# First layer of a two-part transformer: x first, modulation weights by column halves, projection pieces in between

## The chip, the core and the metric

The kernel runs on one core of a Trainium2 chip. The core has five engines that run side by side, each through its own instructions in order: TensorE (PE in the profile) multiplies matrices into PSUM, VectorE (DVE) and ScalarE (ACT) work element by element on SBUF and PSUM, GpSimd (POOL) on SBUF alone, and SyncE (SP) issues the loads and stores, which 16 DMA engines carry out. Semaphores order the engines. PE loads one operand as weights (PEld in the profile) and streams the other.

The metric is the device time of the whole program in microseconds, median of the runs. Lower is better.

## The reference

Six transformer layers over one sequence of 512 rows of 1024 float32 values. The first four are modulated by a condition c; the change concerns the start of the first of them:

```python
cond = jax.nn.silu(c)
for i in range(DEPTH):
    mod = (cond @ w_mod[i] + b_mod[i])[:, None, :]
    shift, scale, gate = jnp.split(mod, 3, axis=-1)
    h = rms_norm(x, norm_pre_g[i]) * (1.0 + scale) + shift
    ...
    o = gla_mixer(h, ...)
    ...
    x = x + gate * rms_norm(o, norm_post_g[i])
```

```python
def gla_mixer(h, w_in, w_a2, b_a, g_head, w_out):
    q, k, v, z, a_low = jnp.split(h @ w_in, [GLA_KD, 2 * GLA_KD, 2 * GLA_KD + GLA_VD, 2 * GLA_KD + 2 * GLA_VD], axis=-1)
    log_a = jax.nn.log_sigmoid((a_low @ w_a2 + b_a)) / GLA_NORMALIZER
    ...
```

`w_mod[0]` has 1024 rows and 3072 columns: 1024 of shift, 1024 of scale, 1024 of gate. `w_in` has 3088 columns; the values v of head 0 are columns 1024 to 1279. Two further layers (a second block with its own context sequence) follow and are not touched.

## The kernel before

One program computes everything, with x resident as four tiles of 128 rows. A planner at build time puts each engine's instructions in order from their place in the program and from simulated times; it also hands out the buffers of a pool, tag by tag in the order of the program (`NBUF`: 28 buffers of 4 KB per partition under "t4", 10 under "t2", 5 raw weight pieces "wr", 4 each of their high and low parts "wh" and "wl").

`setup` (L139) loads the identity and a few columns, makes silu(c) (`condition`), and loads the shift and scale columns of `w_mod[0]` as 16 tiles of 128 rows by 1024 columns (512 KB each, k the block of rows, v shift or scale). x (`load_x`, four tiles of 512 KB) is issued after the eighth of them (L157). For each tile four matmuls with the condition as weights (L164; the profile counts eight) accumulate one row of shift and one of scale in PSUM. These rows are copied (L170), turned into columns by PE (L173) and joined with bias and norm weight (L178 to L182): `m` holds a scale and a shift for each of the 1024 features.

`first_block` (L2172) then normalises the four x tiles (`normed`, L518: squares on ScalarE, root on POOL, scaling on DVE and ScalarE) and calls `prenorm`'s step (L482). It transposes each pair or single tile on PE (L501), applies scale and shift out of PSUM (L507, L509) and splits the result into a high part that a fast matmul format holds and a low remainder (`split`, L254: copy on ScalarE, subtraction on DVE or POOL, L257). H, the normalised input with features on partitions, is eight blocks k of 128 features by 512 rows, high and low.

Then `gla` (L628) begins. It loads the head gain `gh` (L631) and projects head 0's values (`values`, `proj_tok` L288): four pieces of weights, each of two blocks k by 256 columns (256 KB, rows of 1 KB), each split into high and low; for each piece and each of four row tiles six matmuls (L310 to L312: high by high, high by low, low by high). That makes 96. Next are the decay (`gla_decay`, L667: three matmuls for each k with 16 columns, L675 to L677) and the queries and keys of head 0 (`proj_T`, L358 to L360).

Generators yield to a driver (`drain`, L423), which at each yield gives background work 0.6 of a step: the modulation rows of later layers (`mods`, L380; eight matmuls a tile, L393). `ADV = 1` lets the first piece of the values run ahead of the constants of the whole program (`consts`, L2153: some thirty small loads and two transposes of stacked columns, L228).

Of the kernel before, what the change touches and what calls it, by code (L numbers as in the profile page):

```python
# [21 lines left out]
D = 1024  # L22
# [54 lines left out]
class Core:  # L77
    def __init__(self, ctx, tc, A):
        self.ctx, self.tc, self.nc, self.A = ctx, tc, tc.nc, A
        pool = lambda name, bufs, **k: ctx.enter_context(tc.tile_pool(name=name, bufs=bufs, **k))  # L80
        self.cp = pool("const", 1)
        self.wp = pool("w", 3)
        self.mx = pool("mx", 2)
        self.sm = pool("sm", 4)
        self.dp = pool("dram", 1, space=DRAM)
        self.ps = pool("ps", 1, space=PSUM)
        self.turn = {}
        self.n = 0
        self.ph, self.nlo = "", {}
        self.bg, self.rate, self.owed = {"m": [], "c": []}, {"m": MRATE, "c": 0}, {"m": 0, "c": 0}  # L90
        self.two = "c_2" in A
        self.share = False
        self.sk = ""

# [44 lines left out]
    def setup(self):  # L139
# [13 lines left out]
        w = [self.t("t4", [128, D]) for _ in range(16)]  # L153
        for i, x in enumerate(w):
            k, v = i // 2, i % 2
            nc.sync.dma_start(x, A["w_mod"][0][k * 128:(k + 1) * 128, v * D:(v + 1) * D])
            if i == 7:  # L157
                self.load_x()
        pad = self.cond["c"]
        ps = [self.psA() for _ in range(2)]  # L160
        for i, x in enumerate(w):
            k, v = i // 2, i % 2
            for g in range(4):
                nc.tensor.matmul(ps[v][g * 32:(g + 1) * 32, :256], pad[:, k, :], x[:, g * 256:(g + 1) * 256],  # L164
                                 start=(k == 0), stop=(k == 7))
        m = self.small("mcol", [128, 16], bufs=3)
        bias = self.col("b_mod0", 16)
        for v in (1, 0):
            sb = self.t("t1", [128, 256])
            nc.vector.tensor_copy(sb, ps[v][:, :256])  # L170
            pt = self.psA()
            for h in range(2):
                nc.tensor.transpose(pt[:, h * 128:(h + 1) * 128], sb[:, h * 128:(h + 1) * 128], self.ident)  # L173

            col = pt[:, :256].rearrange("p (h g r) -> p g h r", h=2, r=32)[:, :, :, 0]
            o = m[:, 8 - 8 * v:16 - 8 * v].rearrange("p (g h) -> p g h", h=2)
            bv = bias[:, v * 8:v * 8 + 8].rearrange("p (g h) -> p g h", h=2)
            nc.vector.tensor_tensor(o, col, bv, op=ALU.add)  # L178
            if v:
                pre = self.small("pre0", [128, 8], bufs=1)  # L180
                nc.vector.tensor_scalar(pre, self.col("pre0", 8), 32.0, None, ALU.mult)
                nc.vector.scalar_tensor_tensor(m[:, 0:8], m[:, 0:8], 1.0, pre, ALU.add, ALU.mult)  # L182
        self.m0 = m
# [104 lines left out]
    def proj_tok(self, H, nt, W, K, c0, n, out, r0=0, each=None, inturn=False, lead=1, wide="pp"):  # L288
# [42 lines left out]
        for g in groups:  # L331
            ws = [(k0, nk, self.weights(W, r0 + k0, nk, c0, n)) for k0, nk in g]
# [295 lines left out]
    def gla(self, H, j, O):  # L628
        nc, A = self.nc, self.A
        W = A["gla_w_in"][j]  # L630
        gh = self.bcast(A["gla_g_head"][j].rearrange("h d -> (h d)"), 1024, "t4")  # L631
        nc.vector.tensor_scalar(gh, gh, 0.5, None, ALU.mult)
# [9 lines left out]
        for h in range(4):  # L642
            v = []
            if h == 0:

                yield from values(h, v)
                yield from self.gla_decay(H, j, b)
            o = []
# [1523 lines left out]
    def first_block(self, dst=None):  # L2172
        A, x = self.A, self.x
        H, step = self.prenorm(x, 4, self.m0)
        for t, xn in enumerate([self.normed(x(t)) for t in range(4)]):
            step(t, xn)
        if ADV == 0:
            self.consts()
        yield
        for i in range(4):  # L2180
# [3 lines left out]
            if i % 3 == 0:  # L2184
                gen = self.phase("gla", self.gla(H, i // 3, O))
                if i == 0 and ADV:

                    for _ in range(ADV):
                        next(gen)
                        yield  # L2190
# [32 lines left out]
ADV = 1  # L2223
# [69 lines left out]
```

## Time and profile before

| | us |
|---|---|
| median of 3 runs | 3271.91 |
| lowest, highest | 3269.6, 3280.09 |
| the profiled execution's own time | 3273.38 |
| its span in the profile | 3271.6 |
| PE busy in the span | 3099.9 |
| mean granted clock of PE | 0.975 of 2.4 GHz |

The profile is one execution. Its times are microseconds from the start of the span, single instructions in nanoseconds. In the tables by stages the engines stand in the order PE, PEld, DVE, ACT, POOL, each with its count. An engine that is busy is not always fast: a matmul's duration is modelled, and the distance between the starts of two matmuls says more of PE's pace. PEclk is the clock that was granted to PE in a stretch, 1.00 being 2.4 GHz and 0.50 being 1.2 GHz. A timeline merges equal neighbours and counts them (x8). Behind "<-" stands what an engine waited for.

### The profile page before, as it was taken

The page shows a single profiled execution, that of the slowest core. Times are in us where ns is not written, and L with a number is a line of the kernel's source. Part 1 is how long each engine was busy: PE and PEld are TensorE (multiplying, and loading weights), DVE is VectorE, ACT ScalarE, POOL GpSimd, SP SyncE. Part 2 cuts the span into 40 slices and gives each one's busy share as a digit, 9 for nine tenths or more (in the row PEclk, how much of TensorE's full clock was granted, in tenths as well). Part 3 has the DMA queues.
Part 4 walks back from the last instruction along what each step waited for, and adds up shares of the span by engine and source line. Part 5 has one row for each costly group of instructions (what it writes and reads, how often), then busy time and mean ns, then how long its engine had stood idle before and what let it go on. Part 6 is the DMA issues. An engine that isn't in the chain of part 4 may idle for free.

```text
span 3271.6 us, 61127 instructions
## 1 busy us (share of the span) xinstructions
PE 3099.9 (95%) x23487; PEld 2650.2 (81%) x23487; DVE 1691.7 (52%) x3554; ACT 1458.9 (45%) x3173; POOL 1306.4 (40%) x1312
## 2 busy tenths in 40 slices
PE   7999999999999999989999999899999989999998
PEld 4878889878877778878887789898888877888887
DVE  2744564454555564666897757651112468641112
ACT  3424544354544543345544544453323447643323
POOL 2544453232212345344543113554445341154445
PEclk9999999999989999999999999999999999999999
DMA  7355645754435625354564335353333330043332
GB/s 239 91 152 171 212 132 165 235 164 133 134 117 169 191 76 150 113 160 128 164 171 130 109 86 144 114 160 94 100 123 110 109 90 2 24 142 97 97 123 90
DMA packets 477420, 426.25 MB, mean 130 GB/s; under 512 B 108038, under 2 KB 421609, under 8 KB 477129
## 3 DMA queue, kind: packets, MB, share of 16 engines
q1 hardware_dynamic: 477129, 422.35, 43.0%
q8 instruction: 185, 3.03, 0.4%
q14 instruction: 106, 0.87, 0.1%
HBM read 383.66 MB, written 38.03 MB: 129 GB/s over the span
## 4 chain that ended last, share of the span: by engine, by line
PE 74%; DVE 10%; DMA 5%; ACT 4%; issue 3%; POOL 3%; SPq 1%; POOLq 0%; DVEq 0%; ACTq 0%
PE ffn.pp L359 6%; PE ffn.pp L358 6%; PE ffn.pp L360 6%; PE mods.pa L393 3%; PE out.pp L310 2%; PE out.pp L311 2%; PE out.pp L312 2%; PE ffn.pa L312 2%; PE ffn.pa L311 2%; PE ffn.pa L310 2%; DMA mods.wm<-in_w_mod_dram 2%; PE fox.pp L312 1%; PE fox.pp L311 1%; PE fox.pp L310 1%; PE sgu.pp L310 1%
## 5 line engine op out<-in xcount | busy, mean ns | idle before, releaser
L257 POOL TENSOR_TENSOR ffn.wl<-ffn.wr,ffn.wh 128x512 fp32r<-128x512 f32 x258 | 332.8, 1293 | 345.6 <-ACT ffn.wh L256 345.5
L256 ACT ACTIVATE ffn.wh<-ffn.wr 128x512 fp32r<-128x512 f32 x258 | 162.5, 631 | 348.3 <-PE ffn.pp L360 144.6
L358 PE MATMUL ffn.pp<-pre.t,ffn.wh 128*128 128x512 f32 x672 | 261.6, 389 | 0.0
L359 PE MATMUL ffn.pp<-pre.t,ffn.wl 128*128 128x512 f32 x672 | 261.4, 389 | 0.0
L360 PE MATMUL ffn.pp<-pre.t,ffn.wh 128*128 128x512 f32 x672 | 261.4, 389 | 0.0
L598 DVE SCALAR_TENSOR_TENSOR ffn.t<-ffn.t,ffn.pp 128x512 f32<-128x512 f32 (+1 forms) x66 | 39.4, 597 | 243.9 <-ACT ffn.t L597 243.9
L257 POOL TENSOR_TENSOR gla.wl<-gla.wr,gla.wh 128x512 fp32r<-128x512 f32 x66 | 86.9, 1317 | 162.1 <-ACT gla.wh L256 148.2
L310 PE MATMUL gla.pp<-gla.wh,pre.t 128*128 128x256 f32 x512 | 150.6, 294 | 0.8 <-ACT gla.t L651 0.4
L311 PE MATMUL gla.pp<-gla.wl,pre.t 128*128 128x256 f32 x512 | 149.9, 293 | 0.0
L312 PE MATMUL gla.pp<-gla.wh,pre.t 128*128 128x256 f32 x512 | 149.4, 293 | 0.5 <-DVE pre.t L257 0.4
L359 PEld LDWEIGHTS ffn.pp<-pre.t,ffn.wl 128*128 128x128 f32 x672 | 126.1, 188 | 26.3
L360 PEld LDWEIGHTS ffn.pp<-pre.t,ffn.wh 128*128 128x128 f32 x672 | 126.1, 188 | 26.1
L358 PEld LDWEIGHTS ffn.pp<-pre.t,ffn.wh 128*128 128x128 f32 x672 | 126.1, 188 | 26.0
L257 POOL TENSOR_TENSOR ffn.cwl<-ffn.cwr,ffn.cwh 128x512 fp32r<-128x512 f32 x44 | 60.8, 1382 | 213.8 <-ACT ffn.cwh L256 188.7
L393 PE MATMUL mods.pa<-mods.wm,cond_c 128*32 128x256 f32 x1408 | 122.5, 402 | 16.0 <-DMA mods.wm<-in_w_mod_dram 15.6
L1140 DVE SCALAR_TENSOR_TENSOR ffn.t<-ffn.t,ffn.pp 128x512 f32<-128x512 f32 (+1 forms) x66 | 39.4, 597 | 176.2 <-PE ffn.pp L360 175.5
L256 ACT ACTIVATE ffn.cwh<-ffn.cwr 128x512 fp32r<-128x512 f32 x132 | 82.9, 632 | 104.6 <-PE ffn.pp L360 39.6
L310 PE MATMUL sgu.pp<-sgu.wh,pre.t 128*128 128x256 f32 x384 | 112.6, 293 | 6.9 <-DVE gdnp.at L1267 6.0
L311 PE MATMUL ffn.pa<-ffn.wl,ffn.t 128*128 128x512 f32 x304 | 118.3, 389 | 0.0
L312 PE MATMUL ffn.pa<-ffn.wh,ffn.t 128*128 128x512 f32 x304 | 118.3, 389 | 0.0
L310 PE MATMUL ffn.pa<-ffn.wh,ffn.t 128*128 128x512 f32 x304 | 112.7, 389 | 0.0
L312 PE MATMUL sgu.pp<-sgu.wh,pre.t 128*128 128x256 f32 x384 | 110.8, 289 | 1.3 <-DVE pre.t L257 1.1
(823 smaller groups left out, 10719.7 us busy)
## 6 DMA issues: line engine op xcount, KB each, us to landing
mods.wm<-in_w_mod_dram SPq DMA_DIRECT2D x176, 512.0 KB
gla.wr<-in_gla_w_in_dram SPq DMA_DIRECT2D x96, 256.0 KB
ffn.wr<-in_w_ffn_gate_dram SPq DMA_DIRECT2D x88, 256.0 KB
ffn.wr<-in_w_ffn_up_dram SPq DMA_DIRECT2D x88, 256.0 KB
ffn.wr<-in_w_ffn_down_dram SPq DMA_DIRECT2D x88, 256.0 KB
fox.wr<-in_fox_w_in_dram SPq DMA_DIRECT2D x64, 256.0 KB
sgu.wr<-in_sgu_w_in_dram SPq DMA_DIRECT2D x48, 256.0 KB
out.res_x<-out.t SPq DMA_DIRECT2D x24, 512.0 KB
```

Source lines behind the costliest of these rows:

```text
L256: nc.scalar.activation(hi, src, AF.Copy)
L257: (lo_eng or nc.vector).tensor_tensor(lo, src, hi.bitcast(F32), op=ALU.subtract)
L310: nc.tensor.matmul(o, H.hi(kk, s), w[0][:, k], start=(kk == 0 and first), stop=False)
L311: nc.tensor.matmul(o, H.hi(kk, s), w[1][:, k], start=False, stop=False)
L312: nc.tensor.matmul(o, H.lo(kk, s), w[0][:, k], start=False, stop=(kk == K - 1 and last))
L358: nc.tensor.matmul(o, wh[:, k], H.hi(kk), start=(kk == 0), stop=False)
L359: nc.tensor.matmul(o, wl[:, k], H.hi(kk), start=False, stop=False)
L360: nc.tensor.matmul(o, wh[:, k], H.lo(kk), start=False, stop=(kk == K - 1))
L393: nc.tensor.matmul(ps[g * 32:(g + 1) * 32, :256], pad[:, j, :], ws[j][:, g * 256:(g + 1) * 256], start=(j == 0), stop=(j == 7))
L598: nc.vector.scalar_tensor_tensor(dst, dst, 1.0, z, ALU.add, ALU.mult)
L1140: nc.vector.scalar_tensor_tensor(f, sg, 0.5, o[1], ALU.mult, ALU.mult)
```

## The change

x is loaded ahead of the weights. The weights of shift and scale are loaded by column halves: a tile holds, for one block k, 512 columns of shift and the same 512 of scale (two rows of 2 KB on each partition, 512 KB in all). `setup` issues half 0, two pieces of the value projection, half 1, two more pieces. It normalises x, computes the columns of half 0 (`mods0`, `mods1`), and in between transposes the normalised x unscaled into `xT` (four tiles, eight copies out of PSUM by ScalarE and DVE in turn). The first two pieces are split there.

`first_block` makes the four blocks k of half 0 from `xT` (`norm0`: high part on ScalarE with scale and shift, the same in full on DVE, the difference on DVE or POOL), runs the value projection's first two pieces between the modulation matmuls of half 1, then makes the other four blocks and splits the last two pieces. After one yield come the constants and the rest. `proj_tok` takes pieces out of `self.early` before it loads any. The head gain's load in `gla` moves behind the decay.

```diff
--- before.py
+++ after.py
@@ -91,6 +91,7 @@
         self.two = "c_2" in A
         self.share = False
         self.sk = ""
+        self.early = []
 
     def nm(self, s):
         self.n += 1
@@ -150,37 +151,90 @@
         self.columns("cols0", [("c", r(A["c"]), 8), ("b_mod0", r(A["b_mod"][0:1, 0:2 * D]), 16),
                                ("pre0", r(A["norm_pre_g"][0:1]), 8)])
         self.condition("c", ("c",))
-        w = [self.t("t4", [128, D]) for _ in range(16)]
-        for i, x in enumerate(w):
-            k, v = i // 2, i % 2
-            nc.sync.dma_start(x, A["w_mod"][0][k * 128:(k + 1) * 128, v * D:(v + 1) * D])
-            if i == 7:
-                self.load_x()
-        pad = self.cond["c"]
-        ps = [self.psA() for _ in range(2)]
-        for i, x in enumerate(w):
-            k, v = i // 2, i % 2
+        self.load_x()
+        src = A["w_mod"][0][:, 0:2 * D].rearrange("(k p) (v n) -> k p v n", p=128, v=2)
+
+        def half(i):
+            w = [self.t("t4", [128, 2, 512]) for _ in range(8)]
+            for k in range(8):
+                nc.sync.dma_start(w[k], src[k][:, :, i * 512:(i + 1) * 512])
+            return w
+
+
+        w = half(0)
+        W = A["gla_w_in"][0]
+        raws = []
+
+        def pieces(*ks):
+            for k0 in ks:
+                raws.append(self.w("wr", 2, 256, F32))
+                nc.sync.dma_start(raws[-1], W[k0 * 128:(k0 + 2) * 128, 1024:1280].rearrange("(k p) n -> p k n", p=128))
+
+        pieces(0, 2)
+        self.w0 = half(1)
+        pieces(4, 6)
+        self.m0 = self.small("mcol", [128, 16], bufs=3)
+        self.pre0 = self.small("pre0", [128, 8], bufs=1)
+        nc.vector.tensor_scalar(self.pre0, self.col("pre0", 8), 32.0, None, ALU.mult)
+        xn = [self.normed(self.x(t)) for t in range(4)]
+        ps = self.psA()
+        self.mods0(ps, w, 0, 6)
+        self.xT = [self.t("t4", [128, 2, 512]) for _ in range(4)]
+        for k in range(8):
+            pt = self.psP()
+            for t in range(4):
+                nc.tensor.transpose(pt[:, t * 128:(t + 1) * 128], xn[t][:, k * 128:(k + 1) * 128], self.ident)
+            (nc.vector.tensor_copy if k % 2 else nc.scalar.copy)(self.xT[k // 2][:, k % 2], pt)
+        self.mods0(ps, w, 6, 8)
+        self.mods1(ps, 0)
+        self.raws = raws
+        self.early = [self.parts(raws.pop(0), "gla") for _ in range(2)]
+
+    def parts(self, raw, ph):
+
+        hi, lo = (self.w(tag, raw.shape[1], raw.shape[2]) for tag in ("wh", "wl"))
+        self.split(hi, lo, raw, self.lo_engine(ph))
+        return hi, lo
+
+    def mods0(self, ps, w, k0, k1):
+
+        for k in range(k0, k1):
             for g in range(4):
-                nc.tensor.matmul(ps[v][g * 32:(g + 1) * 32, :256], pad[:, k, :], x[:, g * 256:(g + 1) * 256],
-                                 start=(k == 0), stop=(k == 7))
-        m = self.small("mcol", [128, 16], bufs=3)
+                self.nc.tensor.matmul(ps[g * 32:(g + 1) * 32, :256], self.cond["c"][:, k, :],
+                                      w[k][:, g // 2, g % 2 * 256:g % 2 * 256 + 256], start=(k == 0), stop=(k == 7))
+
+    def mods1(self, ps, i):
+
+        nc, m = self.nc, self.m0
+        sb = self.t("t1", [128, 256])
+        nc.vector.tensor_copy(sb, ps[:, :256])
+        pt = self.psA()
+        for h in range(2):
+            nc.tensor.transpose(pt[:, h * 128:(h + 1) * 128], sb[:, h * 128:(h + 1) * 128], self.ident)
+
+        col = pt[:, :256].rearrange("p (h g r) -> p g h r", h=2, r=32)[:, :, :, 0]
         bias = self.col("b_mod0", 16)
         for v in (1, 0):
-            sb = self.t("t1", [128, 256])
-            nc.vector.tensor_copy(sb, ps[v][:, :256])
-            pt = self.psA()
-            for h in range(2):
-                nc.tensor.transpose(pt[:, h * 128:(h + 1) * 128], sb[:, h * 128:(h + 1) * 128], self.ident)
-
-            col = pt[:, :256].rearrange("p (h g r) -> p g h r", h=2, r=32)[:, :, :, 0]
-            o = m[:, 8 - 8 * v:16 - 8 * v].rearrange("p (g h) -> p g h", h=2)
-            bv = bias[:, v * 8:v * 8 + 8].rearrange("p (g h) -> p g h", h=2)
-            nc.vector.tensor_tensor(o, col, bv, op=ALU.add)
-            if v:
-                pre = self.small("pre0", [128, 8], bufs=1)
-                nc.vector.tensor_scalar(pre, self.col("pre0", 8), 32.0, None, ALU.mult)
-                nc.vector.scalar_tensor_tensor(m[:, 0:8], m[:, 0:8], 1.0, pre, ALU.add, ALU.mult)
-        self.m0 = m
+            c = 8 - 8 * v + 4 * i
+            bv = bias[:, v * 8 + 4 * i:v * 8 + 4 * i + 4].rearrange("p (g h) -> p g h", h=2)
+            nc.vector.tensor_tensor(m[:, c:c + 4].rearrange("p (g h) -> p g h", h=2), col[:, 2 * v:2 * v + 2], bv, op=ALU.add)
+        s = slice(4 * i, 4 * i + 4)
+        nc.vector.scalar_tensor_tensor(m[:, s], m[:, s], 1.0, self.pre0[:, s], ALU.add, ALU.mult)
+
+    def norm0(self, H, i):
+
+        nc, m = self.nc, self.m0
+        old, self.ph = self.ph, "pre"
+        for k in range(4 * i, 4 * i + 4):
+            if k % 2 == 0:
+                for part in (H.h, H.l):
+                    part[k // 2] = self.t("t4", (128, 2, 512), F32R)
+            x, a, b = self.xT[k // 2][:, k % 2], m[:, k:k + 1], m[:, 8 + k:9 + k]
+            hf = self.t("t2", [128, 512])
+            nc.scalar.activation(H.hi(k), x, AF.Identity, bias=b, scale=a)
+            nc.vector.tensor_scalar(hf, x, a, b, ALU.mult, ALU.add)
+            (nc.vector if k % 2 else nc.gpsimd).tensor_tensor(H.lo(k), hf, H.hi(k).bitcast(F32), op=ALU.subtract)
+        self.ph = old
 
     def setup2(self):
         nc, A = self.nc, self.A
@@ -329,7 +383,7 @@
 
             groups = groups[:-2] + [ks[-2:]]
         for g in groups:
-            ws = [(k0, nk, self.weights(W, r0 + k0, nk, c0, n)) for k0, nk in g]
+            ws = [(k0, nk, self.early.pop(0) if self.early else self.weights(W, r0 + k0, nk, c0, n)) for k0, nk in g]
             for t in range(nt):
 
                 for k0, nk, w in ws:
@@ -628,8 +682,6 @@
     def gla(self, H, j, O):
         nc, A = self.nc, self.A
         W = A["gla_w_in"][j]
-        gh = self.bcast(A["gla_g_head"][j].rearrange("h d -> (h d)"), 1024, "t4")
-        nc.vector.tensor_scalar(gh, gh, 0.5, None, ALU.mult)
         b = []
 
         def values(h, v):
@@ -645,6 +697,8 @@
 
                 yield from values(h, v)
                 yield from self.gla_decay(H, j, b)
+                gh = self.bcast(A["gla_g_head"][j].rearrange("h d -> (h d)"), 1024, "t4")
+                nc.vector.tensor_scalar(gh, gh, 0.5, None, ALU.mult)
             o = []
             yield from self.proj_T(H, 512, W, 8, [h * 128, 512 + h * 128], o)
             qT, kT = self.t("t2", [128, 512]), self.t("t2", [128, 512])
@@ -2171,23 +2225,24 @@
 
     def first_block(self, dst=None):
         A, x = self.A, self.x
-        H, step = self.prenorm(x, 4, self.m0)
-        for t, xn in enumerate([self.normed(x(t)) for t in range(4)]):
-            step(t, xn)
-        if ADV == 0:
-            self.consts()
-        yield
+        H = Split([None] * 4, [None] * 4, 2)
+        self.norm0(H, 0)
         for i in range(4):
             sc = self.scr["a", i]
             O = self.newO()
             self.context_rate(2 * i)
             if i % 3 == 0:
                 gen = self.phase("gla", self.gla(H, i // 3, O))
-                if i == 0 and ADV:
-
-                    for _ in range(ADV):
+                if i == 0:
+
+                    ps = self.psA()
+                    for k in (0, 4):
                         next(gen)
-                        yield
+                        self.mods0(ps, self.w0, k, k + 4)
+                    self.mods1(ps, 1)
+                    self.norm0(H, 1)
+                    self.early = [self.parts(raw, "gla") for raw in self.raws]
+                    yield
                     self.consts()
                 yield from gen
                 W = A["gla_w_out"][i // 3]
@@ -2220,7 +2275,6 @@
 LO = {'': 'p', 'pre': 'ppd', 'c': 'ddp', 'cgdnp': 'd', 'cmlap': 'd', 'gla': 'ppd', 'oddq': 'pdd', 'coddkv': 'pd', 'gdnp': 'ppd', 'oddkv': 'pdd', 'out': 'ddp', 'cout': 'pd', 'mlap': 'ppd', 'fox': 'pdd', 'cmla': 'd'}
 PREA = (3,)
 MRATE, MB = 0.6, 2
-ADV = 1
 PRI = 100
 DOWN = ((512, 512), (512, 256, 256))
 LEAD = (1, 1, 1, 1, 2)
```

## Rows read from the trace of the kernel before

**Rows 1.** The page, part 1: busy us, share of the span, instructions.

```profile
PE 3099.9 (95%) x23487; PEld 2650.2 (81%) x23487; DVE 1691.7 (52%) x3554; ACT 1458.9 (45%) x3173; POOL 1306.4 (40%) x1312
```

**Rows 2.** Stages: us; busy us of five engines; PEclk, DMA share, GB/s.

```profile
0.00:44.00 44.00, 24.34 (x163) 9.95 (x164) 9.24 (x27) 13.37 (x31) 9.49 (x28) 0.97 0.83 300
44.00:63.00 19.00, 16.55 (x111) 15.01 (x110) 10.16 (x29) 8.91 (x23) 9.58 (x10) 0.80 0.72 195
63.00:93.00 30.00, 30.00 (x170) 18.76 (x168) 13.72 (x24) 17.17 (x21) 6.41 (x5) 1.00 0.53 153
```

**Rows 3.** Timeline of PE, 31 to 63 us: start us, us, instruction.

```profile
31.86 1.08 PE L164 MATMUL .pa<-.t,cond_c 128*32 128x256 f32 x8 [0.24 <-DMA .t<-in_w_mod_dram]
...
44.38 0.41 PE L310 MATMUL gla.pp<-gla.wh,pre.t 128*128 128x256 f32 x1
44.59 0.41 PE L311 MATMUL gla.pp<-gla.wl,pre.t 128*128 128x256 f32 x1
...
48.27 0.28 PE L311 MATMUL gla.pp<-gla.wl,pre.t 128*128 128x256 f32 x1
48.39 0.28 PE L312 MATMUL gla.pp<-gla.wh,pre.t 128*128 128x256 f32 x1
...
57.13 0.28 PE L228 MATMUL .pa<-ident,.t 95*128 95x95 f32 x1 [2.01 <-DMA .t<-in_gdn_conv_dram]
...
60.51 1.08 PE L393 MATMUL mods.pa<-mods.wm,cond_c 128*32 128x256 f32 x8
...
63.00 0.40 PE L675 MATMUL gla.pa<-pre.t,gla.wh 128*16 128x512 f32 x1
```

**Rows 4.** Timeline of SP's queue, 6 to 51 us: load issues.

```profile
6.37 4.14 SPq L62 DMA_DIRECT2D .t<-in_x_dram  x4
...
11.46 9.29 SPq L156 DMA_DIRECT2D .t<-in_w_mod_dram  x8
...
24.25 0.33 SPq L2141 DMA_DIRECT2D tri<-in_k_tri_dram  x1
...
36.75 0.43 SPq L1938 DMA_DIRECT2D gqk<-in_gqa_k_norm_dram  x1
...
37.23 0.94 SPq L279 DMA_DIRECT2D gla.wr<-in_gla_w_in_dram  x2
...
48.60 1.47 SPq L279 DMA_DIRECT2D gla.wr<-in_gla_w_in_dram  x3
...
50.12 0.49 SPq L224 DMA_DIRECT2D .t<-in_norm_pre_g_dram  x1
```

**Rows 5.** Three short stretches, same columns as Rows 2.

```profile
12.00:16.00 4.00, 3.40 (x32) 0.60 (x24) 0.00 (x0) 0.00 (x0) 0.00 (x0) 1.00 1.03 410
...
46.00:48.00 2.00, 2.00 (x11) 2.00 (x10) 0.69 (x3) 1.98 (x6) 2.00 (x2) 0.50 0.22 43
...
50.00:52.00 2.00, 2.00 (x19) 2.00 (x19) 2.00 (x3) 0.82 (x3) 2.00 (x3) 1.00 1.06 296
```

**Rows 6.** Timeline of ACT: first and last of its work on x.

```profile
16.59 0.63 ACT L525 ACTIVATE .sq<-.t 128x512 f32<-128x512 f32 x1 [12.37 <-DMA .t<-in_x_dram]
...
23.98 0.72 ACT L531 ACTIVATE .t<-.t,.rr 128x512 f32<-128x512 f32 x1 [0.41 <-POOL .rr L539]
```

**Rows 7.** Groups by shape, 0 to 64 us: busy us, mean ns, idle before.

```profile
L501 PE MATMUL pre.pa<-ident,.t 128*128 128x128 f32 x32 | 7.0, 403 | 3.8 <-ACT pre.t L507 3.8
...
L257 POOL TENSOR_TENSOR pre.t<-pre.t,pre.t 128x512 fp32r<-128x512 f32 x3 | 4.0, 1340 | 2.9 <-ACT pre.t L256 2.9
```

**Rows 8.** Timeline of DVE: the last step of the scale columns.

```profile
34.42 0.17 DVE L182 SCALAR_TENSOR_TENSOR .mcol<-.mcol,.pre 128x8 f32<-128x8 f32 x1
```

**Rows 9.** Chain that ended last, 38 to 70 us: start us, us, what.

```profile
38.73 6.27 DMA gla.wr<-in_gla_w_in_dram
...
68.72 0.57 PE mods.pa L393 x8
```

**Rows 10.** The page, part 6: the background tiles' loads.

```profile
mods.wm<-in_w_mod_dram SPq DMA_DIRECT2D x176, 512.0 KB
```

## The prediction

> **What bounds the kernel now.** I read the page's busy line first [rows 1]: TensorE (PE) is busy 95% of the span, every other engine half of it or less. So time is won only where PE is idle or slow, and the page leaves 171.7 us of idle PE in all. The table by stages comes second [rows 2]: from 0 to 44 us PE is busy 24.3 us, from 44 to 63 us 16.6 of 19 us at a mean clock of 0.80, from 63 to 93 us all of 30 us. Behind the first projection the change moves only the head gain's load, so all it can win lies ahead of 63.0 us, where the low-rank decay projection (L675) starts behind the last matmul of head 0's values (L310 to L312) [rows 3].
>
> Third comes the load queue [rows 4]: eight weight tiles, x, eight weight tiles, then one projection piece. SP issues x, the ninth large load, at 6.37 us and spreads four issues over 4.1 us, eight over 9.3: one for each large load that lands, with eight under way. The tiles come at 410 GB/s, 1.28 us for 512 KB, with the DMA engines full (1.03) [rows 5]. So x reaches ScalarE at 16.59 us [rows 6] and the last modulation weights reach PE at 31.86 us [rows 3]. Only then are the columns made (L170 to L182), the rows transposed and modulated in one long chain, and the first full run of value matmuls is under way at 44.4 us. Pieces 2 to 4 of the projection are issued at 37.23 us or later, behind thirteen small constant loads (L2141 to L1938) [rows 4]. From 46 to 48 us the DMA engines move 43 GB/s [rows 5], bandwidth that the start could have used.
>
> Fourth, PE's rows at single instructions [rows 3]: value matmuls follow each other every 0.21 us at 44.4 us and every 0.12 us at 48.3 us. The granted clock is 0.50 from 46 to 48 us, that is 1.2 GHz, and 1.00 from 50 to 52 us, 2.4 GHz [rows 5]: it rose after some four busy microseconds. PE then idles 2.0 us until the loads of the constant columns land (L228, 57.13 us), and at 60.5 us eight background matmuls take 1.08 us, 0.57 at 68.7 us [rows 3, 9]: the clock had fallen again.
>
> **The change, part by part.**
>
> *Loads.* The order becomes x, column half 0 (8 tiles), two pieces, column half 1 (8 tiles), two pieces. These are the 11 MiB of now (x, weights, four pieces). What is new is rows of 2 KB instead of 4 KB, which no row of the trace times: the bounds are 410 GB/s (4 KB rows) and 296 GB/s (50 to 52 us, when three pieces with rows of 1 KB move) [rows 4, 5]. I take 355, about half way, as 2 KB lies between both in size. x lands at 6.4 to 10.3 us (four tiles at 1.28). Half 0 (4.19 MB) takes 11.8 us and ends at 22.1; two pieces (0.52 MB at 296) end at 23.9; half 1 ends at 35.7 us. By the bounds 32.0 and 40.5 us.
>
> The Trainium skill ("DMA: Bandwidth & Descriptors", "Specifications") gives about 358 GB/s as the limit of loads from HBM into one core; the 410 above is over it, so for 4 KB rows the measurement decides. For 2 KB rows no run here shows it; by the page's figure half 1 would end at 35.5 us (an estimate from that page).
>
> *Normalising x.* ScalarE works on the four tiles from 16.59 to 24.70 us now [rows 6]. The same 8.1 us from 6.5 us on end at 14.6 us. The work is moved, not changed, and the weight loads cover it: free.
>
> *Transposes.* 32 on PE as before, 7.0 us busy [rows 7]; new are eight evictions into xT, four on ScalarE and four on VectorE, for which the nearest row is a ScalarE activation of the same shape, 0.63 us [rows 6]. They run from 14.6 to about 22 us, while half 0 lands: free. Without that cover they would cost at most 8 x 0.63 / 2 = 2.5 us.
>
> *Columns and rows of half 0.* The last tile's matmuls take 1.1 us, the columns 1.6 us (32.94 to 34.59 [rows 3, 8]); then come per k an activation of 0.63 and a subtraction, 1.34 us on POOL for even k [rows 6, 7]: 2.0 us to the first complete row. Value matmuls of k 0 to 3 can start at 22.1 + 4.7 = 26.8 us instead of 44.4. They are 48 of 96: 10.2 us at half clock, 5.8 at full. Beside them PE has half 1's weights, 1.08 us a tile at half clock, 0.57 at full. By 26.8 us two of these tiles are done, so 10.2 + 6 x 1.08 = 16.7 us of work at half clock are left; with the clock up after four of them, as at 48 us, the other 12.7 take 7.0, and it ends at 37.8 us, a little after the load's 35.7 + 1.1.
>
> *Rows of half 1.* Columns 1.6 and first rows 2.0 give 41.4 us. PE stands still about 3 us there, and the 2.0 us before 57.13 were followed by half clock, so I take four microseconds at 0.21 (19 matmuls) and 29 at 0.12: 7.5 us. The values end at 48.9 us, against 63.0 now: 14.1 us. By the bounds: 410 GB/s and full clock give 32.0 + 1.1 + 3.6 + 5.8 = 42.5 us; 296 GB/s and half clock in this half 40.5 + 1.1 + 3.6 + 10.2 = 55.4 us.
>
> *What PE did meanwhile before.* One background tile (L393, 1.08) and two column transposes (L228, 0.28 and much the same) ran ahead of 63.0 us [rows 3]; they come later now: 1.6 us back. Net 12.5 us, bounds 18.9 and 6.0.
>
> *What is moved past what.* The constants' loads now stand behind all 24 large loads on SP. The last large load is issued when the sixteenth lands, near 27 us; eight small ones follow, one per landing, until 37.5 us; the other five need about 0.5 us each on SP (L1938: 0.43 [rows 4]), so the decay weights are issued near 40 us. In the trace of before a piece took 6.3 us from its issue to ScalarE [rows 9]: 46.3 us, split at most 0.63 + 1.34 later, at 48.3. The cover is the second half of the values (41.4 to 48.9), and it just does; beyond it each microsecond late costs one. The head gain's load (gh) moves behind the decay, where its reader is far off: nothing. The splits of four pieces are the same instructions as now. Two yields fewer reach the background work, 1.2 of its steps: below 1.1 us, either way.
>
> From 63 to 93 us PE has filler for the whole decay chain [rows 2], so I take the rest of the kernel as shifted whole. The profiled execution's own time is 3273.38 us (span 3271.6), 1.5 above the median of 3271.91. 3273.4 - 12.5 = 3260.9 for such an execution, **3259 us** beside the median.
>
> **Rivals.**
>
> *The small loads take the removed wait's place.* For it: PE's queue runs in order, a transpose of the constant columns already stops it for 2.0 us, and their loads are issued (50.12 us) only once the last row buffers are taken [rows 3, 4]; now that falls between 41 and 46 us. Against it: PE has 7.5 us of values there. If transposes or decay weights hold PE until 55 us, 6.1 us of the 12.5 go: 3265.5 us.
>
> *PE stays at half clock.* At 85% busy (3.40 of 4 us) the load stage of before ran eight such matmuls in 1.08 us throughout, against 0.57 at 68.7 us; the clock printed for that stretch, 1.00, doesn't fit these durations [rows 3, 5, 9]. If nothing raises it, half 1's weights end at 26.8 + 16.7 = 43.5, the values at 43.5 + 3.6 + 10.2 = 57.3 us: 5.7 - 1.6 = 4.1 us won, 3268 us. Against it: transposes and value matmuls fill the gaps between tiles. The Trainium skill ("TensorE: Matmul & The Clock Gate", "Part 1: The HAM clock gate") says that the clock is low by default and that activity raises it; 44 to 48 us agrees, and by it both gaps here would cost clock again.
>
> *Slower: the background tiles lose their places.* All later instructions are put in order by a planner that starts from this stage, and the 176 tiles of L393 [rows 10] fill PE's waits by their place between yields, which moves by 1.2 steps. A tile that covered a wait costs its 0.57 us where it covers none. To end 0.3% slower (9.8 us), 12.5 + 9.8 = 22.3 us must be lost: 40 of 176 tiles. At 42 it is 3283 us. Against it: the shift is one step, not a new rate.
>
> *The change doesn't do what it says:* the planner may put half 1's weights ahead of the first value matmuls. Then the rows of half 1 are made while these run, and the end is the same within 2 us; this is inside the forecast.
>
> **Numbers.** Forecast 0.64, small loads 0.17, half clock 0.11, slower 0.08. A measurement here tells about 0.3% from no change, 9.8 us, or 3262.1 us: of the forecast 0.56 lie beyond it (values end before 51.6 us) and 0.08 short of it, and the two middle rivals are within it. Faster 0.56, same 0.36, slower 0.08. The forecast's own bounds are 3253 to 3266; the range takes in both middle rivals and some re-planning on either side: 3247 to 3274.
>
> **What would show it.** Right: x at ScalarE near 6.5 us, first value matmuls near 27, decay matmuls near 49, and from there on the same stages 12 to 14 us earlier. Wrong: half 1's weights still landing after 41 us (2 KB rows), value matmuls 0.21 us apart past 46 us, L228 or the decay weights on PE's waits after 46 us, or an early gain that is gone some layers on.

## The result and the profile after

The changed kernel took 3300.03 us (median; 3297.75 to 3303.71), the kernel before 3271.24 beside it: a ratio of 1.0084 with an interval of 1.0063 to 1.0104. It is 29 us **slower**; the forecast was 12 us faster. The profiled execution took 3298.96 us, its span is 3297.2.

The busy line of the page of after, to be held against [rows 1]:

```profile
PE 3115.8 (94%) x23487; PEld 2663.8 (81%) x23487; DVE 1691.2 (51%) x3551; ACT 1460.8 (44%) x3169; POOL 1302.0 (39%) x1308
```

TensorE (PE) runs the same number of matmuls, is busy 15.9 us longer, and idles 181.4 us instead of 171.7. So of the 25.6 us between the two spans 9.7 are new idle time and 15.9 are the same matmuls run slower, at a lower clock: the mean granted clock is 0.969 against 0.975.

**The start did much of what was forecast.** First the table by stages of after, in the form of [rows 2] (window, its length, then busy us of PE, PEld, DVE, ACT, POOL; clock; DMA share; GB/s); then ScalarE's first work on x; then rows of PE and SyncE (start, length, engine, line, idle before and what ended it):

```profile
12.00:16.00 4.00, 3.77 (x28) 1.94 (x32) 0.74 (x2) 2.56 (x6) 0.76 (x2) 1.00 1.05 400
16.00:24.00 8.00, 6.58 (x74) 3.73 (x70) 3.93 (x8) 3.50 (x6) 1.11 (x1) 1.00 1.06 380
24.00:36.00 12.00, 10.37 (x57) 7.48 (x58) 6.18 (x7) 3.56 (x5) 4.30 (x4) 0.57 1.04 350
...
57.00:83.00 26.00, 26.00 (x116) 16.37 (x115) 9.91 (x28) 14.25 (x19) 2.56 (x2) 0.88 0.43 132
83.00:94.00 11.00, 6.50 (x39) 4.73 (x37) 7.88 (x15) 2.58 (x4) 3.57 (x3) 0.69 0.57 185
94.00:125.00 31.00, 31.00 (x222) 25.91 (x215) 20.38 (x33) 10.95 (x20) 16.79 (x17) 1.00 0.49 140
```

```profile
5.81 0.63 ACT L579 ACTIVATE .sq<-.t 128x512 f32<-128x512 f32 x1 [1.61 <-DMA .t<-in_x_dram]
```

```profile
25.14 0.39 PE L364 MATMUL gla.pp<-.wh,pre.t 128*128 128x256 f32 x1 [0.20 <-ACT pre.t L234]
...
38.68 1.93 PE L203 MATMUL .pa<-.t,cond_c 128*32 128x256 f32 x32
...
42.96 0.39 PE L364 MATMUL gla.pp<-.wh,pre.t 128*128 128x256 f32 x1 [1.36 <-ACT pre.t L234]
...
44.32 0.38 PE L366 MATMUL gla.pp<-.wh,pre.t 128*128 128x256 f32 x1 [0.62 <-POOL pre.t L236]
...
46.73 0.58 PE L366 MATMUL gla.pp<-.wh,pre.t 128*128 128x256 f32 x1 [1.44 <-DVE nea L1985]
...
55.97 0.27 PE L282 MATMUL .pa<-ident,.t 95*128 95x95 f32 x1 [1.80 <-DMA .t<-in_mla_kv_norm_dram]
56.55 0.33 PE L282 MATMUL .pa<-ident,.t 60*128 60x60 f32 x1 [0.31 <-DMA .t<-in_gdn_conv_dram]
56.81 0.61 PE L729 MATMUL gla.pa<-pre.t,gla.wh 128*16 128x512 f32 x1
```

```profile
54.34 0.24 SPq L278 DMA_DIRECT2D .t<-in_mla_kv_norm_dram  x1
```

(Line numbers of after lie 54 higher from the projections on: L364 to L366 are L310 to L312 of before, L282 is L228, L729 is L675, L447 is L393, L706 is L652.) x is at ScalarE at 5.8 us (forecast 6.5), the first value matmul runs at 25.1 (26.8), the loads are through by about 36 (35.7). Half 1's values start at 43.0 us (41.4) and meet two more short waits; the constants' columns then hold PE for 1.80 and 0.31 us, and the decay starts at 56.8 instead of 63.0 us: 6.2 us of head start, where 14.1 were forecast ahead of the put-off work.

**Then it is lost.** The window 83 to 94 us, full in before [rows 2], has 4.5 us of idle PE and a clock of 0.69 in after. The next table is worked out from the two traces: the start of each matmul in after less its start in before, main-path matmuls matched one by one, the median over a stretch of before's time. Zero is level with before; beside it stand four experiments that are told below.

```
us of before      90-125  250-350  500-550  610-640  950-1000  1210-1250  1310-1380  1500-1525
after               0.8      2.0      1.5     10.5      10.6      12.0       18.7       25.8
steps_late          2.9      3.3      6.9     15.8      18.1      23.9       32.0       40.7
yields_back        -3.5     -7.5     -5.7     -4.9      -4.8      -5.2       -4.6        2.6
x_first            -2.3     -6.1     -5.7     -5.1      -3.7      -6.4       -5.6       -3.9
kt_on_scalar       -7.3     -1.4      0.7      7.9       3.9       4.3        7.1       13.6
```

The loss comes in steps at a few places, the last of them a little after the 176 background tiles are used up (near 1400 us). From 1500 us to the end the lag stays near 25.8 us. In the instruction lists as built, the order differs between the two kernels on all five engines, for the last time near 1640 us of before.

**Two of the steps, followed to an instruction.** The first, in the chain of waits of after at 80 to 90 us (start, length, what):

```profile
82.60 0.08 DVE gla.t L754
...
82.94 4.37 DVE gla.t L754 x7
87.31 0.59 DVE gla.t L706
87.91 0.14 issue
88.04 2.05 PE glah.pa L765 x8
```

and VectorE (DVE) in before, at the same work:

```profile
86.08 0.69 DVE L652 COPY gla.t<-gla.pp 128x512 f32<-128x512 f32 x1 [0.28 <-PE gla.pp L360]
88.49 4.76 DVE L700 TENSOR_TENSOR_SCAN gla.t<-gla.t,gla.t 128x128 f32<-128x128 f32 x8 [1.72 <-ACT gla.t L696]
```

In before the copy of k transposed (L652, in after L706) is ahead of eight scans; in after it is behind them. PE waits 4.50 us for that one copy, and here the head start is gone. (In gain_back and kt_on_scalar, below, PE doesn't wait so long here, and the head start is gone by 500 us all the same.)

The second, at 606 us: SyncE's issues, after first, then before.

```profile
600.79 0.37 SPq L333 DMA_DIRECT2D gdnp.cwr<-in_w_in_even_dram  x1
601.25 0.46 SPq L1357 DMA_DIRECT2D gdn_tok_ctx<-gdnp.t  x1
601.76 0.42 SPq L515 DMA_DIRECT2D .t<-.gg  x1
602.30 0.89 SPq L443 DMA_DIRECT2D mods.wm<-in_w_mod_dram  x2
```

```profile
595.80 0.42 SPq L461 DMA_DIRECT2D .t<-.gg  x1
596.33 1.15 SPq L389 DMA_DIRECT2D mods.wm<-in_w_mod_dram  x2
597.68 0.38 SPq L279 DMA_DIRECT2D gdnp.cwr<-in_w_in_even_dram  x1
```

In before the background tile's load goes out ahead of the next layer's weights (cwr), in after behind them, and that load had to wait for VectorE (SyncE's waits of after, 594 to 612). The tile then has no cover; chain of after, PE's rows there, and the stretch of 30 us around the tile as windows, before (587:617) and after (596:626):

```profile
SPq L333 <- DVE gdnp.t L1355: 4.3, 1, 4.3
```

```profile
602.30 7.59 DMA mods.wm<-in_w_mod_dram
609.94 1.08 PE mods.pa L447 x8
611.02 0.51 PE out.pp L364
```

```profile
609.94 1.08 PE L447 MATMUL mods.pa<-mods.wm,cond_c 128*32 128x256 f32 x8 [3.79 <-DMA mods.wm<-in_w_mod_dram]
...
611.54 0.41 PE L366 MATMUL out.pp<-out.wh,sgu.t 128*128 128x256 f32 x1
611.76 0.41 PE L364 MATMUL out.pp<-out.wh,sgu.t 128*128 128x256 f32 x1
```

```profile
587.00:617.00 30.00, 29.63 (x265) 27.12 (x264) 11.23 (x25) 12.35 (x33) 7.37 (x7) 1.00 0.77 255
```

```profile
596.00:626.00 30.00, 25.87 (x207) 23.22 (x206) 10.77 (x22) 12.01 (x31) 8.67 (x8) 0.89 0.69 227
```

PE idles 3.79 us before the tile, the clock falls after it (matmuls 0.21 us apart at 611.5), and 58 matmuls fewer are run in 30 us. That the order of these two loads is the cause is read from the rows; no run put them back alone.

### The profile page after: what moved, and what is told of

The parts are those of the page before. It is cut to its first block, busy times and chain, and to the rows that moved or that the text cites. A ratio compares the mean times of both kernels' runs of the same rounds, so it can differ in the third digit from the quotient of the medians.

```text
span 3297.2 us, 61112 instructions
## 1 busy us (share of the span) xinstructions
PE 3115.8 (94%) x23487; PEld 2663.8 (81%) x23487; DVE 1691.2 (51%) x3551; ACT 1460.8 (44%) x3169; POOL 1302.0 (39%) x1308
## 4 chain that ended last, share of the span: by engine, by line
PE 75%; DVE 10%; DMA 5%; ACT 4%; POOL 2%; issue 2%; SPq 1%; DVEq 0%; POOLq 0%; ACTq 0%
PE ffn.pp L413 6%; PE ffn.pp L412 6%; PE ffn.pp L414 5%; PE mods.pa L447 3%; PE out.pp L364 2%; PE out.pp L366 2%; PE out.pp L365 2%; PE ffn.pa L364 2%; PE ffn.pa L365 2%; PE ffn.pa L366 2%; DMA mods.wm<-in_w_mod_dram 2%; PE fox.pp L364 1%; PE fox.pp L365 1%; PE fox.pp L366 1%; PE sgu.pp L364 1%
## 5 line engine op out<-in xcount | busy, mean ns | idle before, releaser
L310 ACT ACTIVATE ffn.wh<-ffn.wr 128x512 fp32r<-128x512 f32 x258 | 162.5, 631 | 348.0 <-PE ffn.pp L414 142.7
L652 DVE SCALAR_TENSOR_TENSOR ffn.t<-ffn.t,ffn.pp 128x512 f32<-128x512 f32 (+1 forms) x66 | 39.4, 596 | 243.6 <-ACT ffn.t L651 243.5
L364 PE MATMUL gla.pp<-gla.wh,pre.t 128*128 128x256 f32 x480 | 141.4, 295 | 3.5 <-ACT gla.t L705 2.0
L447 PE MATMUL mods.pa<-mods.wm,cond_c 128*32 128x256 f32 x1408 | 132.2, 403 | 12.5 <-DMA mods.wm<-in_w_mod_dram 12.4
L311 POOL TENSOR_TENSOR gla.wl<-gla.wr,gla.wh 128x512 fp32r<-128x512 f32 (+1 forms) x63 | 82.9, 1318 | 148.9 <-ACT gla.wh L310 137.0
L365 PE MATMUL gla.pp<-gla.wl,pre.t 128*128 128x256 f32 x480 | 141.5, 295 | 0.0
L366 PE MATMUL gla.pp<-gla.wh,pre.t 128*128 128x256 f32 x480 | 140.5, 293 | 0.4 <-POOL pre.t L311 0.3
L310 ACT ACTIVATE ffn.cwh<-ffn.cwr 128x512 fp32r<-128x512 f32 x132 | 83.0, 632 | 108.1 <-PE ffn.pp L414 43.8
L366 PE MATMUL ffn.pa<-ffn.wh,ffn.t 128*128 128x512 f32 x304 | 118.3, 389 | 0.0
L364 PE MATMUL sgu.pp<-sgu.wh,pre.t 128*128 128x256 f32 x384 | 112.7, 294 | 3.3 <-DVE gdnp.at L1321 3.0
L366 PE MATMUL sgu.pp<-sgu.wh,pre.t 128*128 128x256 f32 x384 | 111.7, 291 | 1.9 <-DVE pre.t L311 1.2
L364 PE MATMUL ffn.pa<-ffn.wh,ffn.t 128*128 128x512 f32 x304 | 112.7, 389 | 0.0
```

The costliest lines, as they stand in the source:

```text
L310: nc.scalar.activation(hi, src, AF.Copy)
L311: (lo_eng or nc.vector).tensor_tensor(lo, src, hi.bitcast(F32), op=ALU.subtract)
L364: nc.tensor.matmul(o, H.hi(kk, s), w[0][:, k], start=(kk == 0 and first), stop=False)
L365: nc.tensor.matmul(o, H.hi(kk, s), w[1][:, k], start=False, stop=False)
L366: nc.tensor.matmul(o, H.lo(kk, s), w[0][:, k], start=False, stop=(kk == K - 1 and last))
L447: nc.tensor.matmul(ps[g * 32:(g + 1) * 32, :256], pad[:, j, :], ws[j][:, g * 256:(g + 1) * 256], start=(j == 0), stop=(j == 7))
```

## The experiments

Three things of the change could reorder or delay the later work: the start itself (loads, rows by halves), two yields fewer, so that the background tiles come 1.2 steps later (P, for place), and the head gain's load (G). Each ran by itself.

**yields_back.** The changed kernel with both yields given back:

```
         self.norm0(H, 0)
+        yield
...
+                        if k == 0:
+                            yield
```

> The changed kernel, with the two yields given back that its start swallows (after the first four blocks of rows, and after the first piece of the values), so that the background work has the same step at the same place of the program as in the kernel before. Theory P (phase: the 1.2 background steps that the change leaves out at the start put all later instructions in another order, and that order costs the time): the lag steps near 600, 1250 and 1400 us go away and the head start of the values stays in part; 3260 to 3275 us. Theory S (start: any other start times make the planner re-order, the phase is nothing special): still slow, 3290 to 3305 us. Theory G (the head gain's load behind the decay costs it): unchanged, 3298 us.

Measured 3275.39 us against 3269.21, ratio 1.0013 (1.0002 to 1.0024). Some 23 of the 29 us are back; what is left is 6 us beside the kernel before. In the table the version leads by 4.6 us until 1380 us and loses 7 us between 1380 and 1500, as after, steps_late and kt_on_scalar do. The time lies 0.4 us above theory P's range.

**gain_back.** The changed kernel with the head gain's load at the head of the layer again:

> The changed kernel, with the head gain's load back at the head of the layer. Theory G: at least half of the loss goes, under 3286 us. Theories P and S: 3293 to 3303 us, like the changed kernel.

Measured 3296.3 us in one execution: within 4 us of the change. G is not the cause.

**steps_late.** The kernel before, nothing changed but the count from which background steps are taken:

```
-        ... self.owed = ..., {"m": 0, "c": 0}
+        ... self.owed = ..., {"m": -1.2, "c": 0}
```

> The kernel before, with its background work 1.2 steps late from the start on and nothing else changed. Theory P: the loss comes without the new start, 3285 to 3305 us, in steps at the same places. Theory S: the start times are as before, so 3268 to 3276 us. Theory G: 3271 us.

Measured 3317.32 us, ratio 1.0144 (1.0129 to 1.0159). A shift by two yields alone costs the kernel before 48 us, with no new start at all, and 12 us more than theory P's upper bound. And it meets the same wait at the same place as the change, 5 us later; the chain of steps_late:

```profile
607.69 7.54 DMA mods.wm<-in_w_mod_dram
615.27 1.08 PE mods.pa L393 x8
```

So P is shown from both sides: giving the place back takes most of the loss away, and moving it alone brings a loss. In the instruction lists as built, steps_late differs from before on all five engines too, for the last time near 1640 us.

**x_first.** The kernel before with x loaded ahead of the weight tiles. In the instruction lists as built, PE, VectorE and POOL keep their order; SyncE's first loads and six of ScalarE's instructions on x change places.

> The kernel before, with x issued ahead of all sixteen weight tiles and nothing else: its normalisation ends some 10 us earlier, but rows can't be modulated before the columns are there, after the last weight tile near 32 us. All theories: 3268 to 3274 us, and the same order of instructions on every engine from the first projection on. A loss of 5 us or more would show that times of the start alone, without another order, cost later.

Measured 3269.23 us. Timed in rounds (x_first_timed):

> The kernel before with x loaded ahead of the 16 weight tiles and nothing else changed, timed in rounds; every engine keeps its instruction order. The weights then end about 5 us later and x comes 5 to 10 us earlier. If the time of a kept order follows the start: within 3 us of before either way (0.999 to 1.001). If even a kept order throws anew: more than 5 us off.

3270.12 against 3270.90, ratio 1.0004 (0.9989 to 1.0018). With the order kept behind the start, x ahead of the weights changes nothing that can be measured: such a shift of start times does not cost by itself. It is a shift of 2.3 us at 90 to 125 us (table), less than the change's, so a larger one is not tested by this run.

**How far and which way.** Does lateness cost, or any other place? The kernel before with counts of -0.6, +0.6 and -3.0, and the changed kernel with the yields and the gain's load back:

> The kernel before with the count for the background steps started at -0.6: every background tile one yield later, half of what the change does, and nothing else changed. Theory L (lateness: tiles that come later cover less and less, steadily): about half of the 48 us of the run with -1.2, 3285 to 3300 us. Theory T (placement: any new place of the tiles sends the planner another way, and the size doesn't follow the shift): no fixed size; a time outside 3285 to 3300 speaks for it, above all one as far off as 3317.

> The kernel before with the count started at +0.6: every background tile one yield EARLIER. Theory L: not slower, 3255 to 3272 us, since what is late in the change is early here. Theory T: slower too, by 8 us or more (3280 to 3315), since the places that the kernel had are only lucky ones.

> The kernel before with the count started at -3.0: five yields, or three whole steps, later. Theory L: more than the 48 us of -1.2, so 3320 to 3390 us. Theory T: somewhere between 3270 and 3320, not more than -1.2 gave.

> The changed kernel with both yields given back and the head gain's load back at the head of the layer: the order of VectorE's instructions then agrees with the kernel before in 3095 of 3227 places, against 2883 with the yields alone. If the 6 us that the version with the yields loses near 1400 us come from that order: 3265 to 3270 us. If they come from the load order and the earlier start: 3272 to 3280, as with the yields alone. In neither case do I expect the 12 us that I forecast, since an earlier start alone with the order of before (x loaded first) gave 3269.

Measured 3289.4, 3274.9, 3306.6 and 3286.1 us, each in one execution, beside 3274.18 for the kernel before. A half step late costs some 15 us, which is inside theory L's range; three steps cost less than 1.2, and with that a steady price of lateness falls. order_back lies above both of its ranges. Half a step early fits neither theory's range and is near level; in rounds (half_step_early_timed) it is 3277.93, ratio 1.0018 (1.0006 to 1.0031), slightly worse:

> The kernel before with every tile one yield earlier, timed in rounds: the order nearest to a free improvement in the looks (3274.9 beside 3274.2). If place 0 is only one of several good ones: 0.999 to 1.002. If place 0 is the best one: 1.0015 or more.

order_back has VectorE's order nearer to before than yields_back (3095 against 2883 places, as its expectation says), and is 11 us slower: an order that is nearer is not therefore better. It is also the new start without the other two parts, and by this one execution 12 us slower than the kernel before, so the new start isn't free of re-ordering either.

**The same shifts with the new start** (yields given back, counts as named):

> The version with the yields given back, its count for the background steps started at +0.6: the partner of half_step_early, which has the start of before and the same place of every tile (3274.9 us). Theory W (the new start is worth its 6 to 12 us, and the order of the later work hides that): 3263 to 3269 us. Theory N (what the new start wins by 60 us is used up by 125 us, whatever the order): 3270 to 3280. One pair tells little; the three pairs of this call are to be read together with the two that are there (no shift: 3275 against 3270; -1.2: 3300 against 3317), as a mean difference: W wants -6 to -12, N wants 0 within what single orders scatter.

> The version with the yields given back, count started at -0.6: the partner of half_step_late (3289.4 us). Theory W: 3277 to 3283 us. Theory N: 3284 to 3295. If the scatter is the planner's, not the start's, the pair may differ by more than 10 us in either direction.

> The version with the yields given back, count started at -3.0: the partner of three_steps_late (3306.6 us). Theory W: 3294 to 3301 us. Theory N: 3302 to 3312. If the loss depends on the place of the tiles alone, this one is slow too, over 3290 us; if it is a matter of chance in each build, it needn't be.

> The version with the yields given back, its count started at +1.2, two yields EARLIER. From the pairs measured (early +0.6: 3274.9 and 3276.4; 0: 3270 and 3275.4; late -0.6: 3289 and 3281; -1.2: 3317 and 3300; -3.0: 3307 and 3299) earlier than 0 costs nothing and later costs 5 to 48: 3268 to 3280 us. Outside it, places earlier than 0 scatter as those later do.

> The version with the yields given back, its count started at +3.0: five yields, three whole steps, earlier. If early places cost nothing: 3266 to 3280 us. If each shift is a new throw, whatever its sign: as for -3.0, 3285 to 3310.

```
count            -3.0     -1.2     -0.6      0       +0.6     +1.2     +3.0
start of before  3306.6   3317.3   3289.4   3270     3274.9     -        -
new start        3299.2   3300.0   3280.6   3275.4   3276.4   3282.0   3282.8
```

(At -1.2 the new start is the change itself. The kernel before's only execution beside the new start at +0.6, -0.6 and -3.0 took 6563.53 us, for a cause that the record doesn't show; it is not used here. Most entries are single executions; those of yields_back lie between 3264 and 3280 us, so differences under 8 us say little.) Both starts have their best place at or near the one that the kernel before had, and later places cost 5 to 47 us with either. Early ones cost 7 at most. So the place is one thing; the new start by itself, down the columns, is worth -7, -17, -9, +5 and +2, on average -5 us with a scatter of 9. Whether it is worth 3 or 10 us these pairs can't tell (theory W and N stay undecided). The early ones of the new start, 3282.0 and 3282.8 us, lie 2 to 3 us above the range in which early places cost nothing.

**kt_on_scalar.** Is the loss a sum of separate waits, each with a cause of its own? The copy behind the wait at 83 us moved to ScalarE, in the changed kernel; the line runs eight times (81 to 1352 us), so all eight copies of k move:

```
-            nc.vector.tensor_copy(kT, o[0][1])
+            nc.scalar.copy(kT, o[0][1])
```

> The changed kernel with one instruction moved: the copy of k transposed (L706) is made by ScalarE instead of VectorE, where it stands behind eight scans in the changed kernel and PE waits 4.50 us for it at 83.5 us. Theory S (the loss is a sum of separate stalls, each from one instruction that the planner put behind another one's wait, and each takes some clock with it): the 4.5 us stall is gone, L765 starts by 84 us instead of 88, and from 95 to 150 us the kernel lies 4 to 8 us ahead of the changed one; the later stalls (606, 638, 1010) need not go, so 3285 to 3297 us. Theory B (bound elsewhere: the scans or the background tiles set the pace there, the wait only shows it): by 125 us nothing is left of it, and the time stays within 3 us of 3299.

Measured 3284.45 us; in rounds (kt_on_scalar_timed) 3287.94 against 3270.90, ratio 1.0058 (1.0039 to 1.0077):

> The changed kernel with the copy of k transposed on ScalarE, timed in rounds beside the kernel before. The single look gave 3284.5 against 3300. If that stands: ratio to the kernel before of 1.003 to 1.006, and about half of the change's loss hangs on the place of this one copy. If the look was a stray: 1.0075 or more.

Beside its own kernel before, the change loses 28.8 us and this version 17.0: some 12 us less by the medians, 8.5 by the two ratios, whose intervals overlap a little (1.0063 to 1.0104 against 1.0039 to 1.0077). Waits of PE from 56 to 125 us (for what; in total, times, longest), after and kt_on_scalar, and the window 83 to 94 of the latter:

```profile
PE glah.pa L765 <- DVE gla.t L706: 4.5, 1, 4.5
```

```profile
PE glah.pa L765 <- ACT gla.t L706: 1.2, 1, 1.2
```

```profile
83.00:94.00 11.00, 11.00 (x96) 8.89 (x94) 9.51 (x18) 4.50 (x7) 5.03 (x5) 1.00 0.67 217
```

The wait shrinks from 4.5 to 1.2 us and the clock stays at 1.00. gain_back has no such wait either: its copy happens to run ahead of the scans (VectorE's rows of gain_back):

```profile
76.41 0.69 DVE L706 COPY gla.t<-gla.pp 128x512 f32<-128x512 f32 x1 [0.54 <-PE gla.pp L414]
77.49 3.70 DVE L754 TENSOR_TENSOR_SCAN gla.t<-gla.t,gla.t 128x128 f32<-128x128 f32 x8 [0.39 <-ACT gla.t L750]
```

Here is the lag behind before once more, now with VectorE's instructions matched, which adds these two runs:

```
us of before         95-125  250-350  500-550  950-1000  1310-1380  1500-1525
after                  -0.8      2.5      2.6      11.3       18.7       25.8
kt_on_scalar           -7.9     -1.2      1.8       4.6        6.5       13.6
kt_on_scalar_timed     -3.9      1.5      1.3       6.2        8.4       15.0
gain_back              -6.0      0.1      2.5       7.5       14.0       20.6
```

At 95 to 125 us all three are 3 to 7 us ahead of the change. At 500 to 550 us 0.1 to 1.3 us of that are left, and gain_back ends at 3296.3 us. So taking the wait at 83 us away has won about 1 us by 550 us: what uses the lead up was not found. The gain of kt_on_scalar comes behind 600 us. Some 4 us of it come at 1290 us (first table, 1210 to 1250 against 1310 to 1380), where the same line of the last such layer stood behind VectorE's L1522 in after, at a cost of 1.4 us of idle PE (waits of after, 1270 to 1300; kt_on_scalar has no such wait there):

```profile
PE gla.pp L364 <- DVE gla.t L706: 1.4, 1, 1.4
```

The wait at 606 us, whose cause was left alone, stays:

```profile
608.76 1.08 PE L447 MATMUL mods.pa<-mods.wm,cond_c 128*32 128x256 f32 x8 [3.40 <-DMA mods.wm<-in_w_mod_dram]
```

So theory S forecast the time (within 1 us) and the lead behind the wait, but not where the gain comes from: the lead is used up as theory B said, only later than 125 us. Eight copies moved and the later order changed with them, so which place gave the rest of the gain stays open. The other steps were not removed one by one.

**yields_and_kt.** The same copy moved in yields_back, where the wait at 83 us isn't there:

> The version with the yields given back (3275.4 us), with the copy of k transposed on ScalarE. Theory S: the stall at 83.5 us isn't there in this order, so little is won at the start; the copy also stands in PE's way near 1290 us in the changed kernel only. 3265 to 3277 us; if it comes under 3265 us it beats the kernel before. Theory B: 3273 to 3278.

Measured 3279.9 us in one execution, above both ranges: no gain. No version here beats the kernel before clear of noise.

## Why the prediction was wrong

**The step that failed** is "Two yields fewer reach the background work, 1.2 of its steps: below 1.1 us, either way". It priced the moved work (1.2 tiles) and not the new order. The planner re-placed instructions on all queues up to some 1640 us, and this measured 23 us (yields_back) to 48 us (steps_late). With it fell "I take the rest of the kernel as shifted whole": PE has filler from 63 to 93 us in before because VectorE's copy came ahead of the scans, and that is a property of the order, not of the stage.

**The slower rival was the right one and badly weighed.** It named the place of the background tiles, at 3283 us with a chance of 0.08. Its mechanism needs correcting too: not 40 tiles that each lose 0.57 us, but steps of 2 to 9 us at a few places (first table). Two were followed to an instruction that lands behind another one's wait, and only one of these is a tile; what makes the others stays open. The argument against it ("the shift is one step, not a new rate") was no argument: half a step (half_step_late) cost 15 us.

**The start, term by term.** Loads: 355 GB/s taken, and 380 (16 to 24 us) and 350 (24 to 36 us, with the pieces) measured; end as forecast. Normalising and transposes: as forecast within 1 us, and the first value matmul comes 1.7 us early. The first half of the values: the sum had the clock up at 30.8 us, but the matmuls stay 0.21 us apart until 35.7 (0.57 in the window 24 to 36), so the half-clock rival came true in part here. The last four tiles of half 1's weights stand behind all of these values on PE (38.68 us) and end at 40.6, where the sum had 37.8 and the rival 43.5. Columns and first rows then take 2.4 us and not 3.6, which hides part of this. Values of half 1: they start 1.6 us late, wait 0.62 us for POOL's and 1.44 us for VectorE's part of a row (I had no waits between rows), and run at half clock from 46.7 to 49.6 us, so they end near 52.6, not 48.9: 3.7 us. Six matmuls of the next projection ran ahead of the decay, 1.6 us of moved work. The small-loads rival came true in part: the constants issued at 54.3 us held PE until 55.97, some 2.6 us with their transposes. 48.9 + 3.7 + 1.6 + 2.6 = 56.8 us, where the decay starts. What was left of the start's gain with the yields given back is 3.5 us (yields_back at 90 to 125), not 12.5.

**Decay weights and gain.** The weights did not hold PE; the constants ahead of them did. Putting the gain's load back won at most 4 us in the one execution of gain_back, so the term of nothing holds within that; the same move is the one difference between yields_back and order_back, where it goes with a loss of 11 us.

## What to carry to other kernels

Where a planner places instructions on in-order queues, price an edit by what it re-orders as well as by what it moves: a change in the count of yields or background steps is an edit of the whole kernel behind it. Keep such counts fixed while testing a change in one stage, or run the shift by itself beside it; here that single control (steps_late) would have told the sign. When a kernel got slower far from the edit, match its matmuls with those of before, look for the steps in the lag, and at each step ask which instruction now stands behind which other one's wait. Then look further on whether what a removed wait wins is kept: here a lead of 3 to 7 us was almost gone by 550 us.

## What the hardware showed that I had not expected

Loads with rows of 2 KB ran at 380 to 400 GB/s, nearly as fast as rows of 4 KB [rows 5]. A PE wait costs more than its length at its place: 3.79 us of idle time at 606 us were followed by matmuls 0.21 us apart, a granted clock of 0.89 over the 30 us, and in sum the changed kernel paid 15.9 us of slower matmuls beside 9.7 us of idle time. "TensorE: Matmul & The Clock Gate" of the Trainium skill ("Part 1: The HAM clock gate") has the clock fall when PE goes idle; the trace agrees at 606 us and at 83 us (0.69). And a kernel's own executions scatter by more than I had taken: the kernel before ran between 3261 and 3279 us in one set of 21.
